# Sevens of w_down moved between the halves: four per column pair in the first, three and none in the second

## The chip, the cores and the metric

The kernel runs on one core of a Trainium2 chip. The metric is the device time of one execution in microseconds; of the kernel before there are three runs. One more execution was recorded by the hardware profiler, and all rows of the trace are from that one. The engines are named as in the profile: PE is TensorE, PEld its weight load, DVE VectorE, ACT ScalarE, POOL GpSimd, SP SyncE (which issues the loads).

## What is computed

A decoder layer for 256 tokens of width 2048, in float32: attention in two groups of heads with a combined input projection and an output projection, then a gated feed-forward part of width 5632. The change touches the last product of the second part, `y = g @ w_down`, and what surrounds it:

```python
h = rmsnorm(x, pre_ffn_g)
u = causal_dwconv(h @ w_up, conv_w, conv_b)          # (256, 11264)
gate, val = split(u, 2)
y = (gelu(gate) * val) @ w_down                      # (256, 5632) @ (5632, 2048)
x = x + rmsnorm(y, post_ffn_g)                       # the output
```

## The kernel before, in words

**Float32 by parts.** Each operand is split into a rounded high part and the low remainder, and a product is three matmuls: high by high, high by low, low by high (`products`, L973 for 512 columns, `mm3`, L284 for 256). The split of a weight block is a cast on ACT (into a `whi` buffer) and a subtraction on DVE (into `wlo`, called a low below): L118 and L121 for a whole load of 512 KB (128x1024), L287 and L288 for half of one (128x512). Loads come through SP's queue into five `raw` buffers; there are five `whi` and five `wlo` buffers too.

**The feed-forward part** runs in two halves of the width 5632, each of 22 row blocks of 128. Per half, first w_up, convolution and gate make 22 tiles `G` (11 rounds `g` of two); then w_down multiplies them. Four column blocks of 512 make the 2048 outputs; they are taken as two pairs, n=0 (blocks 0 and 1) and n=2 (blocks 2 and 3). Two tiles of 128 tokens (t=0, 1) by two column blocks are the four sums of a pair, in PSUM banks b, g (block n) and e, h (block n+1). They are added into `y_sb` by `down` (L963 on DVE; in the second half ACT squares the finished sum, L965, and POOL multiplies the gain; of the first column pair these multiplications are kept in the list `gains` and issued in the second pair).

**Fours and sevens.** A pair of row blocks (index u, 0 to 10) and one column block is a *four*: one load, one split, 12 matmuls. Both column blocks by fours are 24 matmuls. Instead, a *seven* takes the pair of row blocks and both column blocks at once as a 2x2 product of blocks by seven products instead of eight (Strassen's way): 21 matmuls, two loads, seven half splits, four differences of weight blocks on DVE (L1000 to L1003). The sums of activations that it needs are made beside w_up, on POOL, and split into the tile `sums`. Four of its seven products go to banks of their own, `shared` (a, c, d, f), and `fold` adds these into `y_sb` when the last seven of the pair is through. Three of the 11 pairs of row blocks (WIN = 3) are sevens in both column pairs of both halves; the loop over i has 8 turns, each a four for both column blocks, and at i = 0, 2, 4 a seven first, whose second part (`others`) comes after the fours. In the second half's fold three of the adds are on POOL (L1045, L1048, L1050).

**The tail.** In the second half, column block 3 isn't computed in the loop beside block 2 but after it (`tail`): there fours without a seven run through block 3, for the 8 row-block pairs that are no sevens. Its t=0 sum goes on in bank e. Its t=1 sum is made in two halves of 256 columns in two banks of their own, `b1`, so that the first half can be finished while the second is computed. These banks are opened by a matmul (L1108) whose result an ACT copy (L1109) replaces with `y_sb[:, 1, 1536:2048]`, the sum so far; the products L284 then add to it. For the last six row-block pairs the t=1 products are held back to the end, and the weights of two of them lie in the tile `rest`.

**Order.** PE's order is the program's. That of ACT, DVE, POOL and SP is set by a scheduler that goes by its own costs, up to the end of the tail's products, where the written order takes over.

## Time and profile before

| | |
|---|---|
| time, median of 3 runs | 1065.81 us (1065.45 to 1067.0) |
| profiled execution | 1066.15 us |
| its span, first to last instruction | 1064.4 us |
| mean granted TensorE clock | 0.996 |
| busy: PE, PEld | 1050.5 (99%), 913.8 (86%) us |
| busy: DVE, ACT, POOL | 813.9 (76%), 635.7 (60%), 255.6 (24%) us |
| first half's w_down on PE | about 575.9 to 692 us |
| second half's w_down with the tail, on PE | about 932 to 1056 us |
| second half's column pair n=2 without the tail | about 992 to 1026.5 us |
| loads of w_down | 88 of 512 KB, 4.7 us from issue to landing |
| second half's loads of x for the end, `x_end` | 2 of 1 MB, issued at 1022.41 and 1027.74 us |

Times of the trace are in us from the start of the span. A timeline row has start, duration, engine, line and operation, the tile written and those read, the shape, and in brackets how long the engine had been idle before and what it waited for last. A matmul's duration overlaps the next one's; the rate of a row of matmuls is read from start to start. PEclk is the granted clock, 1.00 being the whole. Where rows of one engine overlap (a cast of 1.05 us, and the next starts 0.95 later) the busy time counts the overlap once.

### The profile page before, as it was taken

The numbers are of one execution on the slowest core, as the hardware profiler recorded it, in microseconds if no ns is written. First come the engines' busy times: TensorE is split into PE (matmuls) and PEld (weight loads), VectorE is DVE, ScalarE is ACT, GpSimd is POOL, SyncE is SP. The second block draws the span as 40 slices with busy tenths as digits, with TensorE's granted clock in tenths as the row PEclk, the third lists the DMA queues.
The fourth block names the chain that finished last, engine by engine and source line by source line (L and its number), as shares of the span: only waits on it lengthen the run. The fifth ranks groups of instructions, "written<-read, shape, count | busy, mean of one in ns | idle before, by whom it ended". The sixth has DMA issues, their size and how long they took to land.

```text
span 1064.4 us, 16400 instructions
## 1 busy us (share of the span) xinstructions
PE 1050.5 (99%) x5920; PEld 913.8 (86%) x5920; DVE 813.9 (76%) x1340; ACT 635.7 (60%) x1124; POOL 255.6 (24%) x280
## 2 busy tenths in 40 slices
PE   9999999999999999999999999999999999999987
PEld 7889988888889888888888888888888888888866
DVE  5989868886568887777678887767877777788982
ACT  6776757767548666556565544455655656555650
POOL 3353245440122433112121000014312212102230
PEclk9999999999999999999999999999999999999989
DMA  8645666545866666666664666766666666557572
GB/s 290 191 128 174 181 192 212 173 154 160 298 222 201 220 200 202 190 198 198 193 185 137 213 210 203 243 190 185 182 204 194 196 190 198 156 181 241 162 259 79
DMA packets 165549, 207.09 MB, mean 195 GB/s; under 512 B 6844, under 2 KB 131036, under 8 KB 164444
## 3 DMA queue, kind: packets, MB, share of 16 engines
q1 hardware_dynamic: 165148, 205.65, 62.1%
q8 instruction: 46, 0.75, 0.3%
q10 hardware_dynamic: 320, 0.40, 0.1%
q14 instruction: 35, 0.29, 0.1%
HBM read 201.68 MB, written 4.21 MB: 193 GB/s over the span
## 4 chain that ended last, share of the span: by engine, by line
PE 91%; DVE 4%; issue 2%; ACT 1%; POOL 1%; DMA 1%; DVEq 0%; POOLq 0%; ACTq 0%
PE bank_acc L262 21%; PE bank_acc L973 15%; PE bank_att L262 15%; PE bank_acc L284 13%; PE bank_acc L269 11%; PE bank_att L269 8%; PE bank_att L973 2%; DVE wlo L121 1%; PE bank_att L450 1%; PE bank_att L485 1%; PE bank_att L494 1%; PE bank_acc L881 1%; DVE wlo L288 1%; PE bank_att L496 0%; DMA raw<-in_w_down_dram 0%
## 5 line engine op out<-in xcount | busy, mean ns | idle before, releaser
L121 DVE TENSOR_TENSOR wlo<-raw,whi 128x1024 fp32r<-128x1024 f32 (+3 forms) x333 | 404.6, 1227 | 137.6 <-ACT whi L118 130.7
L118 ACT CAST whi<-raw 128x1024 fp32r<-128x1024 f32 (+3 forms) x332 | 337.9, 1033 | 191.5 <-issue 100.2
L262 PE MATMUL bank_acc<-hT,whi 128*128 128x512 f32 x1024 | 245.6, 392 | 0.0
L262 PEld LDWEIGHTS bank_acc<-hT,whi 128*128 128x128 f32 x1024 | 188.2, 188 | 37.1
L857 POOL TENSOR_TENSOR u<-u,rowf 128x256 f32<-128x256 f32 x88 | 95.5, 1107 | 456.0 <-DVE u L856 453.0
L973 PE MATMUL bank_acc<-whi,G 128*128 128x512 f32 x520 | 167.9, 391 | 0.1
L262 PE MATMUL bank_att<-hT,whi 128*128 128x512 f32 x704 | 165.7, 390 | 0.0
L262 PEld LDWEIGHTS bank_att<-hT,whi 128*128 128x128 f32 x704 | 130.6, 188 | 26.2
L269 PEld LDWEIGHTS bank_acc<-hT,wlo 128*128 128x128 f32 x1024 | 123.4, 188 | 3.2
L269 PE MATMUL bank_acc<-hT,wlo 128*128 128x256 f32 x1024 | 125.7, 278 | 0.0
L973 PEld LDWEIGHTS bank_acc<-whi,G 128*128 128x128 f32 x520 | 98.2, 189 | 20.7 <-DVE y_sb L963 0.5
L973 PE MATMUL bank_acc<-wlo,G 128*128 128x512 f32 x260 | 101.8, 391 | 0.0
L269 PEld LDWEIGHTS bank_att<-hT,wlo 128*128 128x128 f32 x704 | 83.6, 188 | 1.9
L269 PE MATMUL bank_att<-hT,wlo 128*128 128x256 f32 x704 | 83.9, 277 | 0.0
L284 PE MATMUL bank_acc<-whi,oT 128*128 128x512 f32 (+1 forms) x272 | 81.8, 379 | 0.0
L287 ACT CAST whi<-raw 128x512 fp32r<-128x512 f32 x84 | 48.7, 618 | 36.1 <-PE bank_acc L973 21.2
L288 DVE TENSOR_TENSOR wlo<-raw,whi 128x512 fp32r<-128x512 f32 x84 | 60.6, 755 | 11.8 <-ACT whi L287 11.6
L284 PEld LDWEIGHTS bank_acc<-whi,oT 128*128 128x128 f32 x272 | 50.2, 188 | 9.3
L973 PEld LDWEIGHTS bank_acc<-wlo,G 128*128 128x128 f32 x260 | 49.1, 189 | 10.2 <-DVE wlo L121 0.3
L284 PE MATMUL bank_acc<-wlo,oT 128*128 128x512 f32 (+1 forms) x136 | 51.2, 377 | 0.0
L284 PE MATMUL bank_acc<-whi,hT 128*128 128x384 f32 (+1 forms) x192 | 46.9, 323 | 0.0
L859 ACT ACTIVATE yg<-u,cw 128x256 f32<-128x256 f32 x44 | 26.5, 602 | 32.4 <-POOL u L857 32.4
(250 smaller groups left out, 1286.7 us busy)
## 6 DMA issues: line engine op xcount, KB each, us to landing
raw<-in_w_up_dram SPq DMA_DIRECT2D x176, 512.0 KB, 4.5
raw<-in_w_down_dram SPq DMA_DIRECT2D x88, 512.0 KB, 4.7
raw<-in_w_in_dram SPq DMA_DIRECT2D x51, 512.0 KB, 4.9
raw<-in_w_out_dram SPq DMA_DIRECT2D x32, 512.0 KB, 4.7
raw<-in_w_in_dram SPq DMA_DIRECT2D x16, 384.0 KB, 3.3
cb<-c_dram SPq DMA_DIRECT2D x8, 256.0 KB, 4.2
x_sb<-in_x_dram SPq DMA_DIRECT2D x2, 1024.0 KB, 6.3
x_dram<-x_sb SPq DMA_DIRECT2D x2, 1024.0 KB, 5.8
```

The lines of the kernel that those rows point to most:

```text
L118: i1 = act.copy(hi[:, cs], raw[:, cs])
L121: i2 = dve.tensor_tensor(lo[:, cs], raw[:, cs], hi[:, cs].bitcast(F32), op=ALU.subtract)
L262: pe.matmul(b, hi[:, a, m * P:(m + 1) * P], hT[:, kt, 0:512], start=(kt == 0), stop=(last == (0, kt)))
L269: pe.matmul(b[:, 256:512], lo[:, a, m * P:(m + 1) * P], hT[:, u * 4 + a, 0:256], start=False, stop=(last == (1, u * 4 + a)))
L284: pe.matmul(b, a, r[:, cols], start=(first and i == 0), stop=(last and i == 2))
L287: act.copy(hi, src)
L288: dve.tensor_tensor(lo, src, hi.bitcast(F32), op=ALU.subtract)
L450: pe.matmul(sb[e][:, cs], a[r, t * P:(t + 1) * P], b[r, 0:nk], start=(n == 0), stop=(n == 2))
L485: pe.transpose(pb[:, i * P:(i + 1) * P], p[:, e, c:c + P], ident)
L857: pool.tensor_tensor(u[:, 2:258], u[:, 2:258], rowf, op=ALU.mult)
L859: act.activation(y, u[:, 2:258], AF.Identity, bias=cw[:, 3, ch:ch + 1], scale=cw[:, 2, ch:ch + 1])
L973: pe.matmul(b, x, r, start=b not in opened and not i, stop=closes and i == 2)
```

## The change

The number WIN gives way to a table, SEVENS, of the turns i at which a seven runs, for each half and column pair. In the first half there are four sevens in each column pair, at i = 0, 1, 3, 4 of 7 turns; in the second three in n=0 as before, and in n=2 none. So in the second half's n=2 there is no `fold` and no `shared` bank, the loop has 11 turns of one four each, and the tail has 11 row-block pairs instead of 8. The activation sums s1 to s4 all lie in `s` (s1 no longer overwrites a21 in the G tile), which makes their split 512 columns wide instead of 384. The second half's fold has all its adds on DVE, and the gains of the first column pair are issued at the turn of the last seven, or at i = 0 where there is none.

```diff
--- before.py
+++ after.py
@@ -25,7 +25,7 @@
 NEG = -1e30
 FHALF = 22
 HOLD = 6
-WIN = 3
+SEVENS = (((0, 1, 3, 4), (0, 1, 3, 4)), ((0, 2, 4), ()))
 LOW = (14, 4, 4, 4)
 ROOM = 112
 
@@ -908,8 +908,9 @@
         for half in range(2):
             G = [fp.tile([P, 512], F32R, tag="G", bufs=FHALF, name=f"G{j}")[:, 0:512]
                  for j in range(FHALF)]
+            most = max(len(at) for at in SEVENS[half])
             if half:
-                sums = main.tile([P, WIN, 768], F32R, tag="x", name="sums")
+                sums = main.tile([P, 4, 1024], F32R, tag="x", name="sums")
             for g in range(FHALF // 2):
                 c0 = (half * (FHALF // 2) + g) * 256
                 alt = (g + half) % 2
@@ -934,22 +935,23 @@
                     y = conv(bv[m], 44 + c0 // P + m, "yv")
                     dve.tensor_tensor(y, y, gates[m], op=ALU.mult)
                     ys.append(y)
-                if g < WIN:
+                if g < most:
                     if half == 0 and g == 0:
                         for t in range(2):
                             sp.dma_start(x_dram[t * P:(t + 1) * P, :], x_sb[:, t, :])
-                        sums = main.tile([P, WIN, 768], F32R, tag="x", name="sums")
+                        sums = main.tile([P, 4, 1024], F32R, tag="x", name="sums")
                     s = fp.tile([P, 512], F32, tag="s", name="s")
                     (a11, a21), (a12, a22) = [(y[:, 0:P], y[:, P:256]) for y in ys]
-                    pool.tensor_tensor(s[:, P:256], a11, a21, op=ALU.subtract)
-                    pool.tensor_tensor(a21, a21, a22, op=ALU.add)
-                    pool.tensor_tensor(s[:, 0:P], a21, a11, op=ALU.subtract)
-                    pool.tensor_tensor(s[:, 256:384], a12, s[:, 0:P], op=ALU.subtract)
+                    s1, s2, s3, s4 = (s[:, i * P:i * P + P] for i in range(4))
+                    pool.tensor_tensor(s1, a21, a22, op=ALU.add)
+                    pool.tensor_tensor(s2, s1, a11, op=ALU.subtract)
+                    pool.tensor_tensor(s3, a11, a21, op=ALU.subtract)
+                    pool.tensor_tensor(s4, a12, s2, op=ALU.subtract)
                 for m, y in enumerate(ys):
                     gt = G[g * 2 + m]
                     split(gt[:, 0:256], gt[:, 256:512], y)
-                if g < WIN:
-                    split(sums[:, g, 0:384], sums[:, g, 384:768], s[:, 0:384])
+                if g < most:
+                    split(sums[:, g, 0:512], sums[:, g, 512:1024], s)
             if half == 1:
                 rest = main.tile([P, KT, 512], F32R, tag="hT", name="rest")
                 gbf = fp.tile([P, D], F32, tag="gbc", name="gbc_ffn")
@@ -983,7 +985,7 @@
                 split(hi, lo, src)
                 return hi, lo
 
-            def seven(n, u, banks, opened):
+            def seven(n, u, last, banks, opened):
 
                 b, e, g, a, c, d, f = banks
                 k = half * FHALF + u * 2
@@ -991,8 +993,8 @@
                                for m in (n, n + 1)]
                 b11, b21, b12, b22 = (x[:, i * 512:i * 512 + 512] for x in (left, right)
                                       for i in range(2))
-                s2, s3, s4 = [(sums[:, u, i * P:i * P + P], sums[:, u, 384 + i * P:512 + i * P])
-                              for i in range(3)]
+                s1, s2, s3, s4 = [(sums[:, u, i * P:i * P + P],
+                                   sums[:, u, 512 + i * P:640 + i * P]) for i in range(4)]
                 dst = w_parts(UNIT, held=False)
                 w11 = split_512(dst, 0, b11)
                 w22 = split_512(dst, 1, b22)
@@ -1001,7 +1003,6 @@
                 dve.tensor_tensor(b12, b22, b12, op=ALU.subtract)
                 dve.tensor_tensor(b22, b22, b11, op=ALU.subtract)
                 dve.tensor_tensor(b21, b21, b22, op=ALU.subtract)
-                last = u == WIN - 1
                 products(a, parts_of(u * 2, 0), *w11, opened, last)
                 products(b, parts_of(u * 2 + 1, 0), *w21, opened)
                 products(e, s4, *w22, opened)
@@ -1013,7 +1014,7 @@
                     dst = w_parts(UNIT, held=False)
                     t2 = split_512(dst, 0, b22)
                     t4 = split_512(dst, 1, b21)
-                    products(d, parts_of(u * 2, 1), *t1, opened, last)
+                    products(d, s1, *t1, opened, last)
                     products(f, s3, *t3, opened, last)
                     products(c, s2, *t2, opened, last)
                     products(g, parts_of(u * 2 + 1, 1), *t4, opened)
@@ -1042,29 +1043,33 @@
                     act.copy(s, a)
                     dve.tensor_tensor(y11, a, y11, op=ALU.add)
                     dve.tensor_tensor(s, c, s, op=ALU.add)
-                    pool.tensor_tensor(y12, y12, s, op=ALU.add)
+                    dve.tensor_tensor(y12, y12, s, op=ALU.add)
                     dve.tensor_tensor(y12, d, y12, op=ALU.add)
                     dve.tensor_tensor(s, f, s, op=ALU.add)
-                    pool.tensor_tensor(y21, y21, s, op=ALU.add)
+                    dve.tensor_tensor(y21, y21, s, op=ALU.add)
                     dve.tensor_tensor(s, d, s, op=ALU.add)
-                    pool.tensor_tensor(y22, y22, s, op=ALU.add)
+                    dve.tensor_tensor(y22, y22, s, op=ALU.add)
 
             for n in (0, 2):
                 opened = []
                 tail = half and n
-                shared = [bank("att") for _ in range(4)]
+                at = SEVENS[half][n // 2]
+                shared = [bank("att") for _ in range(4 if at else 0)]
                 b, e, g = [bank() for _ in range(3)]
                 h = None if tail else bank()
-                for i in range(FHALF // 2 - WIN):
-                    others = (None if i % 2 or i > 2 * WIN - 2 else
-                              seven(n, i // 2, (b, e, g, *shared), opened))
-                    four(n, WIN + i, (b, g), opened)
+                for i in range(FHALF // 2 - len(at)):
+                    others = None
+                    if i in at:
+                        u = at.index(i)
+                        others = seven(n, u, u == len(at) - 1, (b, e, g, *shared), opened)
+                    four(n, len(at) + i, (b, g), opened)
                     if not tail:
-                        four(n + 1, WIN + i, (e, h), opened)
+                        four(n + 1, len(at) + i, (e, h), opened)
                     if others:
                         others()
-                    if i == 2 * WIN - 2:
+                    if at and i == at[-1]:
                         fold(n, *shared)
+                    if i == max((0, *at)):
                         for args, kw in gains:
                             pool.tensor_tensor(*args, **kw)
                 later_on = None if tail else lambda *args, **kw: gains.append((args, kw))
@@ -1107,7 +1112,7 @@
         for x, cs in zip(b1, halves):
             pe.matmul(x[:, cs], G[0][:, 0:P], G[0][:, 0:256], start=True, stop=False)
             act.copy(x[:, cs], y_sb[:, 1, 1536:2048][:, cs])
-        for u in range(WIN, FHALF // 2):
+        for u in range(len(at), FHALF // 2):
             hi, lo = w_unit(w_rows(w_down, FHALF + u * 2, 2, 1536, 512), 2, 512,
                             keep=(None, [rest[:, c:c + 2, :].rearrange("p a c -> p (a c)")
                                          for c in (4 * (u - LAST), 4 * (u - LAST) + 2)])
```

What moves, in the order of the engines' own programs (shapes without a note are those of the tile written).

ACT at the opening of the tail, before. The L118 rows are casts of weights, the L1109 rows the two copies into the `b1` banks, the L965 rows the squares of the two finished sums of column block 2:

```order
L1042 COPY s<-bank_att 128x512
L118 CAST whi<-raw 128x1024 x5
L118 CAST rest<-raw 128x1024 x2
L118 CAST whi<-raw 128x1024 x2
L1109 COPY bank_att<-y_sb 128x256
L965 ACTIVATE junk,ysq_3954<-y_sb 128x512
L1109 COPY bank_att<-y_sb 128x256
L965 ACTIVATE junk,ysq_3955<-y_sb 128x512
L118 CAST whi<-raw 128x1024 x2
L965 ACTIVATE junk,ysq_3954<-y_sb 128x512
```

And now, where the copies are L1114 and the squares L967:

```order
L118 CAST whi<-raw 128x1024 x9
L118 CAST rest<-raw 128x1024
L118 CAST whi<-raw 128x1024
L118 CAST rest<-raw 128x1024
L118 CAST whi<-raw 128x1024
L967 ACTIVATE junk,ysq_3954<-y_sb 128x512
L1114 COPY bank_att<-y_sb 128x256
L967 ACTIVATE junk,ysq_3955<-y_sb 128x512
L1114 COPY bank_att<-y_sb 128x256
L118 CAST whi<-raw 128x1024 x4
L967 ACTIVATE junk,ysq_3954<-y_sb 128x512
```

Before, one cast stood ahead of the first copy and one square ahead of the second; now a cast and a square stand ahead of the first copy, and the other square ahead of the second. The two casts into `rest` (weights of held-back row-block pairs) have a cast of another unit between them.

DVE in the first half's w_down, column pair n=0, before, from the first seven's second part to the third seven's first difference (L1000 to L1003 are the four differences of a seven, L288 the half lows of sevens, L121 the whole lows of fours):

```order
L121 TENSOR_TENSOR wlo<-raw,whi 128x1024 x2
L288 TENSOR_TENSOR wlo<-raw,whi 128x512 x3
L1000 TENSOR_TENSOR raw<-raw 128x512
L1001 TENSOR_TENSOR raw<-raw 128x512
L121 TENSOR_TENSOR wlo<-raw,whi 128x1024
L1002 TENSOR_TENSOR raw<-raw 128x512
L1003 TENSOR_TENSOR raw<-raw 128x512
L121 TENSOR_TENSOR wlo<-raw,whi 128x1024
L288 TENSOR_TENSOR wlo<-raw,whi 128x512 x4
L121 TENSOR_TENSOR wlo<-raw,whi 128x1024 x2
L288 TENSOR_TENSOR wlo<-raw,whi 128x512 x2
L1000 TENSOR_TENSOR raw<-raw 128x512
```

And now the same stretch, where the differences are L1002 to L1005:

```order
L288 TENSOR_TENSOR wlo<-raw,whi 128x512 x4
L1002 TENSOR_TENSOR raw<-raw 128x512
L121 TENSOR_TENSOR wlo<-raw,whi 128x1024
L1003 TENSOR_TENSOR raw<-raw 128x512
L121 TENSOR_TENSOR wlo<-raw,whi 128x1024
L1004 TENSOR_TENSOR raw<-raw 128x512
L288 TENSOR_TENSOR wlo<-raw,whi 128x512
L1005 TENSOR_TENSOR raw<-raw 128x512
L288 TENSOR_TENSOR wlo<-raw,whi 128x512 x3
L121 TENSOR_TENSOR wlo<-raw,whi 128x1024 x2
L288 TENSOR_TENSOR wlo<-raw,whi 128x512 x2
L1002 TENSOR_TENSOR raw<-raw 128x512
```

The two whole lows of the turn i = 1 that stood ahead of the second seven's half lows and differences are gone from there: its weights follow those of the first at once. Between the second and the third the row is as before.

SP in the second half, before:

```order
L72 DMA raw<-in_w_up_dram 128x4x256 x88
L72 DMA raw<-in_w_down_dram 128x2x512 x42
L1126 DMA x_end<-x_dram 128x2048
L72 DMA raw<-in_w_down_dram 128x2x512 x2
L1126 DMA x_end<-x_dram 128x2048
L1103 DMA out_dram<-y_sb 128x512 x6
```

And now:

```order
L72 DMA raw<-in_w_up_dram 128x4x256 x88
L72 DMA raw<-in_w_down_dram 128x2x512 x23
L1131 DMA x_end<-x_dram 128x2048
L72 DMA raw<-in_w_down_dram 128x2x512 x6
L1131 DMA x_end<-x_dram 128x2048
L72 DMA raw<-in_w_down_dram 128x2x512 x15
L1108 DMA out_dram<-y_sb 128x512 x6
```

The two loads of x_end move from behind 42 and 44 of the second half's 44 loads of w_down to behind 23 and 29.

## The prediction

> **What bounds the kernel now.** I read the page's head and its chain of waits first.
>
> ```profile
> span 1064.4 us, 16400 instructions
> PE 1050.5 (99%) x5920; PEld 913.8 (86%) x5920; DVE 813.9 (76%) x1340; ACT 635.7 (60%) x1124; POOL 255.6 (24%) x280
> PE 91%; DVE 4%; issue 2%; ACT 1%; POOL 1%; DMA 1%; DVEq 0%; POOLq 0%; ACTq 0%
> ```
>
> TensorE carries 91% of the chain, so time goes in two ways: more or fewer products, and places where TensorE stands still. For the second I looked at matmul starts in the two w_down stages, the only ones that the change touches. The first half's stage (575.9 to 692) has no place where starts lie further apart than their neighbours; the second half's has one large place, at the tail's opening (a first matmul L1108 into the bank, then products after a copy L1109). The timeline there, all engines in order of time (start, duration, engine and operation, idle time before it):
>
> ```profile
> 1026.08 3.43 DVE L121 TENSOR_TENSOR rest<-raw,rest 128x1024 fp32r<-128x1024 f32 x2
> 1026.24 2.19 POOL L1050 TENSOR_TENSOR y_sb<-y_sb,s 128x512 f32<-128x512 f32 x1 [0.80 <-DVE s L1049]
> 1026.29 0.39 PE L973 MATMUL bank_acc<-whi,G 128*128 128x512 f32 x1
> 1026.52 0.40 PE L1108 MATMUL bank_att<-G 128*128 128x256 f32 x2
> ...
> 1027.22 0.39 PE L973 MATMUL bank_acc<-whi,G 128*128 128x512 f32 x1
> 1028.46 0.38 ACT L1109 COPY bank_att<-y_sb 128x256 f32<-128x256 f32 x1
> 1028.89 0.39 PE L284 MATMUL bank_att<-whi,G 128*128 128x256 f32 x1 [1.28 <-ACT bank_att L1109]
> 1029.11 0.28 PE L284 MATMUL bank_att<-wlo,G 128*128 128x256 f32 x1
> 1029.23 0.28 PE L284 MATMUL bank_att<-whi,G 128*128 128x256 f32 x1
> ...
> 1030.57 1.27 DVE L963 TENSOR_TENSOR y_sb<-bank_acc,y_sb 128x512 f32<-128x512 f32 x2
> 1031.28 0.63 ACT L965 ACTIVATE junk<-y_sb 128x512 bf16<-128x512 f32 x1 [2.44 <-DVE y_sb L963]
> ...
> 1031.91 0.36 ACT L1109 COPY bank_att<-y_sb 128x256 f32<-128x256 f32 x1
> ...
> 1032.21 0.62 ACT L965 ACTIVATE junk<-y_sb 128x512 bf16<-128x512 f32 x1
> 1032.33 0.58 PE L284 MATMUL bank_att<-whi,G 128*128 128x256 f32 x1 [2.82 <-ACT bank_att L1109]
> ```
>
> The first copy waits for POOL's last add of the fold (1026.24, 2.19 us, so 1028.43). The second stands on ScalarE behind the square L965, and that behind DVE: two lows into `rest` that take 3.43 us while POOL works, another low, then the sum L963 at 1030.57. TensorE waits twice for a copy. The windows, cut where the granted clock changes (length, busy us of PE, PEld, DVE, ACT, POOL, then PEclk, DMA share, GB/s):
>
> ```profile
> 1027.62:1031.03 3.41, 0.62 (x3) 0.41 (x3) 3.41 (x3) 1.13 (x2) 0.81 (x1) 1.00 1.02 371
> 1031.03:1037.86 6.83, 5.53 (x20) 4.95 (x21) 4.33 (x7) 3.62 (x7) 4.26 (x2) 0.50 0.43 177
> 1054.92:1058.33 3.41, 1.56 (x13) 1.35 (x12) 0.98 (x3) 0.47 (x2) 0.55 (x1) 1.00 0.26 92
> 1058.33:1061.75 3.42, 0.00 (x0) 0.00 (x0) 2.39 (x5) 0.00 (x0) 0.00 (x0) 1.00 0.67 245
> ```
>
> After 3.41 us with TensorE busy for 0.62 the clock was at one half for 6.83 us; after 3.41 us with 1.56 busy (second to last row) it was still whole in the next.
>
> The rates, from a row of products without waits near the end:
>
> ```profile
> 1042.70 0.62 PE L973 MATMUL bank_acc<-whi,G 128*128 128x512 f32 x2
> ...
> 1047.46 0.39 PE L973 MATMUL bank_acc<-whi,G 128*128 128x512 f32 x1
> ...
> 1047.68 1.59 PE L284 MATMUL bank_att<-rest,G 128*128 128x256 f32 x12
> 1047.88 0.69 DVE L963 TENSOR_TENSOR y_sb<-bank_acc,y_sb 128x512 f32<-128x512 f32 x1 [9.64 <-PE bank_acc L973]
> ...
> 1049.12 0.28 PE L284 MATMUL bank_att<-whi,G 128*128 128x256 f32 x1
> ```
>
> From 1042.70 to 1047.46 lie 21 starts of 128x512: 0.227 us each. Twelve of 128x256 take 1.44 us: 0.120 each. From the start of a last product (1047.46) to the engine that waits for it (1047.88) it is 0.42.
>
> **The change, part by part.**
>
> *Products.* A seven takes 21 matmuls where two fours take 24. The first half gets two more (-6 matmuls), the second loses three (+9): +3 x 0.227 = **+0.68**. The tail now runs 11 row-block pairs instead of 8, and the three added run their t=1 part as two halves of 256: 36 matmuls at 0.120 (4.32) in the place of 18 at 0.227 (4.09): **+0.23**.
>
> *The fold that ended before the tail.* Column pair n=2 of the second half has no sevens, so no fold: y_sb[1, 1536:2048], which the copies read, is complete since the first half. Both waits as they are go. Counted from start to start: 1027.22 to 1028.89 is 1.67 for a slot of 0.23 (1.44 lost), 0.22 instead of 0.12 for the next (0.10), 1029.23 to 1032.33 is 3.10 for 0.12 (2.98): **-4.52**. With them goes the half clock: from 1032.33 to 1037.86 are 5.53 us, in which a 128x512 took 0.427 where it takes 0.227 (the rows of 0.42 and 0.43 between starts), so 5.53 x 0.200/0.427 = **-2.59**.
>
> ```profile
> 1033.14 0.63 PE L973 MATMUL bank_acc<-whi,G 128*128 128x512 f32 x1
> 1033.57 0.63 PE L973 MATMUL bank_acc<-wlo,G 128*128 128x512 f32 x1
> ```
>
> *The start of n=2.* There the seven of i=0 needed three converted weights at once, and TensorE lost a little: 992.44 to 993.24 is 0.80 for two slots of 0.227 (0.35 lost), 997.57 to 998.39 is 0.82 for three (0.14). With one four per i only one converted unit is needed per 12 x 0.227 = 2.72 us: **-0.49**.
>
> ```profile
> 992.44 0.97 PE L973 MATMUL bank_acc<-whi,G 128*128 128x512 f32 x2
> 993.24 0.40 PE L973 MATMUL bank_acc<-wlo,G 128*128 128x512 f32 x1
> ...
> 997.57 0.61 PE L973 MATMUL bank_acc<-whi,G 128*128 128x512 f32 x2
> ...
> 998.39 0.62 PE L973 MATMUL bank_acc<-whi,G 128*128 128x512 f32 x2
> ```
>
> *What is late next at the opening.* On ScalarE the two copies now stand behind a cast and a square each: cast, square, copy, square, copy. That cast writes a whi buffer that only the last product of n=2 sets free. How long a cast holds ScalarE, from one start to the next:
>
> ```profile
> 994.71 1.04 ACT L118 CAST whi<-raw 128x1024 fp32r<-128x1024 f32 x1
> 995.66 1.65 ACT L287 CAST whi<-raw 128x512 fp32r<-128x512 f32 x3
> ```
>
> Call the start of the opening matmul T (1026.52 above); the last product of n=2 starts at T-0.23. Cast at T-0.23+0.42 = T+0.19; square 0.95 later, T+1.14; copy 0.63 after it (1031.28 to 1031.91), T+1.77; TensorE 0.43 after that (1028.46 to 1028.89), T+2.20. Without a wait it would be there at 1027.22+0.23, T+0.93: 1.27 lost. The second square starts 0.30 after the first copy (1031.91 to 1032.21), T+2.07; its copy T+2.70, TensorE T+3.13. Three matmuls of 256 fill 0.46 of that (0.36 and 0.10 at the restart): 0.47 lost. With 0.10 at the second restart too, both cost 1.27+0.10+0.47+0.10 = **+1.94**. Bounds: nothing, if the cast's buffer is free sooner, and the 4.52 of today, if a load or a low is late; I take the value between because each of its links has a row. DVE's sums of n=2 need the same last product and 0.68 each, less than the cast, so they do not decide.
>
> The half clock should stay away: in a stretch of 3.41 us that holds both waits TensorE stands for 1.27+0.47 and works for about 1.6, as in the row with 1.56 that did not bring it, and far from the 0.62 that did.
>
> *Sevens at consecutive i in the first half* (0 and 1, 3 and 4). Cost nothing, if DVE hides it.
>
> ```profile
> L121 DVE TENSOR_TENSOR wlo<-raw,whi 128x1024 fp32r<-128x1024 f32 x35 | 42.7, 1222 | 16.9 <-ACT whi L118 16.8
> L288 DVE TENSOR_TENSOR wlo<-raw,whi 128x512 fp32r<-128x512 f32 x39 | 26.1, 705 | 8.4 <-ACT whi L287 8.3
> L1000 DVE TENSOR_TENSOR raw<-raw 128x512 f32<-128x512 f32 x5 | 3.4, 684 | 0.0
> 575.90:692.00 116.10, 116.10 (x514) 96.14 (x513) 91.72 (x120) 60.98 (x82) 1.69 (x2) 1.00 0.67 209
> ```
>
> An i with a seven is 21+24 matmuls, 45 x 0.227 = 10.2 us. For it DVE makes two whole lows, seven half ones and four differences: 2 x 1.22 + 7 x 0.705 + 4 x 0.684 = 10.1 us by mean durations, some 9.2 as rows overlap by about 0.1. So it keeps up by 1.0 per i, and an i without a seven (24 matmuls, 5.4 us; two lows, 2.4) gives 3 us back. In the stage as a whole four lows go, 14 half ones and 8 differences come: -4.9 + 9.9 + 5.5 = 10.5 us, so DVE rises from 91.7 of 116.1 us (79%) to some 102 of 114.4 (89%). If it does not keep up, the second of each pair of sevens is late, in four places.
>
> *Transfers and POOL at n=2.* The first x_end load moves up from behind 42 to behind 23 of the second half's 44 w_down loads, the second from 44 to 29, each 1 MB on SP's queue. In the 30 us of n=2 (11 x 2.72) SP must bring 11 loads of 512 KB and these two, 7.9 MB or 260 GB/s; the quoted window around 1029 shows 371 on the same queues. A load behind a waiting x_end has five raw buffers of lookahead, 2.72 us each. I count zero, at worst 1. The four gains on POOL run at the start of n=2, and a low beside a POOL operation took up to 2.3 us (3.43 for two, the first free in part), below 2.72: zero. The Trainium skill, "SBUF — State Buffer", section "Who interferes with whom", says that a DVE operation with two SBUF inputs waits for a whole GpSimd operation that reads SBUF. By that rule a low could wait for a whole operation of POOL, 2.2 us by the row at 1026.24, and end 3.4 after its cast, 0.7 more than a unit: the sum would be up to 1.4 higher for the two or three units beside the gains. The trace agrees that they disturb each other (3.43 us for two lows, where one without POOL takes 1.22).
>
> **Sum:** -4.52 - 2.59 - 0.49 + 0.68 + 0.23 + 1.94 = -4.75. The profiled execution took 1066.15 us, 1.7 around a span of 1064.4: 1061.4 after, with a span of 1059.7. The runs' median is 1065.81, 0.34 less; from there it is 1061.1. I forecast **1061.2 us**.
>
> **Rivals.**
> 1. *The opening costs nothing.* For it: copies, casts and squares are ordered by a scheduler and the cast's buffer may be free earlier. Then 1061.2 - 1.94 = 1059.3. Against: the cast waits for the last product of n=2, and stands ahead of both copies.
> 2. *The clock halves again.* The two new waits lie 0.46 us apart and may fall into one 3.41 us stretch. Such a stretch of 6.83 us costs up to 6.83 x 0.200/0.427 = 3.2; the one above cost 2.6. Time 1061.2 + 2.9 = 1064.1. Against: 1.56 busy kept the clock, and the longest new wait is under half of 2.98. The Trainium skill, "TensorE: Matmul & The Clock Gate", section "A second HAM failure mode: psum-queue depth-cycling", tells of a kernel in which short idle times between groups of matmuls alone made the clock swing. By that rule this rival decides, 1064.1; the trace speaks against it with the 1.56 row.
> 3. *DVE binds in the first half* (the other side). Its idle times in the stage, 16.9 + 8.4 us, stand before lows that wait for ScalarE's cast; they may be no slack but the latency of the chain load, cast, low, difference, cast. Over the 16 i of the two column pairs that is 1.6 us each. An i with a seven then takes DVE 10.1 + 1.6 = 11.7 us, 1.5 over TensorE's 10.2. This decides as soon as that sum passes 10.2, at the second seven of a pair, where no lighter i lies between: four places, 4 x 1.5 = 6.0; and as the late weights hold the buffers of the i behind, these four may be late as well, 12.0. Between them 9.0: 1070.2. For it: the 10.1 by mean durations. Against: today each i with a seven lost nothing, and five raw buffers let the second's loads start early.
> 4. *The opening is as late as now*, by a load behind x_end or a low behind POOL: +4.52 instead of +1.94, and the half clock's 2.6: 1061.2 + 2.6 + 2.6 = 1066.4. Against: DMA is not at its limit there, and no POOL work is left at the opening.
>
> **How the numbers follow.** Forecast 0.66, rival 1 0.10, rival 2 0.11, rival 3 0.08, rival 4 0.05. A difference of over 0.2%, 2.1 us, can be told from no change here: faster is below 1063.7, slower above 1067.9. Faster: 0.66 + 0.10 and a little of rival 2 = 0.78; within: the rest of 2 and all of 4, 0.14; slower: rival 3, 0.08. The forecast's own range is 1059.8 to 1063.2 (the opening between 0.6 and 2.9, a transfer or a low beside POOL up to 1). For 8 in 10 it takes in rival 1 and the near end of rival 2: 1059.1 to 1064.0.
>
> **What would show it.** Right: no halved clock before the kernel's last microseconds; at the opening two waits of TensorE for the copies, 1.0 to 1.5 and 0.3 to 0.6 us, behind cast, square, copy on ScalarE; matmul starts 0.227 apart throughout the first half's w_down and at the start of n=2. Wrong: PEclk below 1 near 1030 (rival 2), starts further apart at the second seven of a pair with DVE idle or late before it (rival 3), a wait above 2 us at the opening with a DMA or DVE named (rival 4). The forecast fails if the first half's stage, 252 x 2 x 0.227 = 114.4 us, takes over 2 us more.

## The result, and the profile after

The changed kernel takes 1061.71 us (median of 5 runs, 1061.52 to 1063.41), the kernel before 1066.04 (5 runs, 1065.45 to 1067.0): 0.9960 of it, 95% interval 0.9949 to 0.9972. The forecast was 1061.2. The profiled execution is the slowest of the five, 1063.41 us with a span of 1061.7; the next paragraphs show where its surplus lies.

The head of the page and the chain of waits of the changed kernel:

```profile
span 1061.7 us, 16409 instructions
PE 1050.2 (99%) x5941; PEld 914.6 (86%) x5941; DVE 803.8 (76%) x1330; ACT 634.0 (60%) x1119; POOL 252.1 (24%) x278
PE 90%; DVE 4%; DMA 2%; issue 2%; ACT 1%; POOL 0%; SPq 0%; DVEq 0%; POOLq 0%; ACTq 0%
```

The shares say next to nothing: TensorE is busy for 0.3 us less, and has 4% on DVE in its chain as before. What changed is seen when the program is cut into stages, each from the start of its first matmul to the start of the next stage's first. "First half" and "second half" below are the two w_down stages, the second with the tail and up to the start of the last matmul; both kernels have nearly the same work in the other rows.

| profiled execution, us | before | after | difference |
|---|---|---|---|
| start to the first w_down matmul | 575.87 | 577.49 | +1.62 |
| first half | 115.60 | 114.62 | -0.98 |
| second half's w_up | 240.68 | 240.68 | 0.00 |
| second half with the tail | 124.05 | 120.65 | -3.40 |
| last matmul to the end | 8.25 | 8.27 | +0.02 |

The +1.62 stands in the first 12 us. The timeline of PE there, after:

```profile
6.50 1.11 PE L309 MATMUL bank_acc<-ident,x_in 128*128 128x128 f32 x4 [0.39 <-DMA x_in<-in_x_dram]
7.27 2.05 PE L225 MATMUL bank_att<-hT,whi 128*128 128x512 f32 x4
```

And before:

```profile
6.13 1.08 PE L309 MATMUL bank_acc<-ident,x_in 128*128 128x128 f32 x4
6.89 1.23 PE L225 MATMUL bank_att<-hT,whi 128*128 128x512 f32 x4
```

Here the first load landed 0.4 us later, and the four matmuls of 128x512 then took 2.05 us instead of 1.23, and the next ones were slow as well. The change touches nothing of it, and the other executions of the changed kernel have spans of 1059.7 to 1060.3. So the executions are compared by stages from here on.

The tail's opening after the change, PE and ACT in order of time (rows of weight loads and of other engines are left out):

```profile
1020.28 0.39 PE L975 MATMUL bank_acc<-whi,G 128*128 128x512 f32 x1
1020.50 0.40 PE L1113 MATMUL bank_att<-G 128*128 128x256 f32 x2
1020.70 1.05 ACT L118 CAST whi<-raw 128x1024 fp32r<-128x1024 f32 x1
...
1021.21 0.39 PE L975 MATMUL bank_acc<-whi,G 128*128 128x512 f32 x1
...
1021.66 0.62 ACT L967 ACTIVATE junk<-y_sb 128x512 bf16<-128x512 f32 x1
...
1022.28 0.36 ACT L1114 COPY bank_att<-y_sb 128x256 f32<-128x256 f32 x1
...
1022.58 0.62 ACT L967 ACTIVATE junk<-y_sb 128x512 bf16<-128x512 f32 x1
1022.70 0.38 PE L284 MATMUL bank_att<-whi,G 128*128 128x256 f32 x1 [1.10 <-ACT bank_att L1114]
1022.92 0.28 PE L284 MATMUL bank_att<-wlo,G 128*128 128x256 f32 x1
...
1023.21 0.36 ACT L1114 COPY bank_att<-y_sb 128x256 f32<-128x256 f32 x1
1023.62 0.39 PE L284 MATMUL bank_att<-whi,G 128*128 128x256 f32 x1 [0.31 <-ACT bank_att L1114]
```

Cast, square, copy, square, copy, as forecast: with T = 1020.50 the cast starts at T+0.20, the square at T+1.16, the copy at T+1.78, PE at T+2.20; the second at T+3.12. And the windows, with the same columns as before:

```profile
1017.00:1024.00 7.00, 5.59 (x28) 4.29 (x27) 6.73 (x7) 5.75 (x10) 1.55 (x2) 1.00 0.75 227
1024.00:1030.00 6.00, 6.00 (x41) 5.43 (x40) 2.71 (x5) 2.11 (x2) 2.00 (x1) 1.00 0.38 145
577.40:692.10 114.70, 114.64 (x506) 94.58 (x505) 98.92 (x137) 64.32 (x91) 1.69 (x2) 1.00 0.66 210
```

The first two rows hold the opening and what follows it, the third the first half. PEclk stays at 1.00 through and behind the opening. In the first half DVE is busy 98.9 of 114.7 us (86%), and TensorE's busy time falls short of the window by 0.06 us. By matmul starts it lost 0.33 there, at one place, the start of the second column pair:

```profile
635.08 0.68 DVE L1005 TENSOR_TENSOR raw<-raw 128x512 f32<-128x512 f32 x1
...
635.68 1.22 DVE L121 TENSOR_TENSOR wlo<-raw,whi 128x1024 fp32r<-128x1024 f32 x1
...
636.81 1.28 DVE L965 TENSOR_TENSOR y_sb<-bank_acc,y_sb 128x512 f32<-128x512 f32 x2
...
637.10 0.95 PE L975 MATMUL bank_acc<-whi,G 128*128 128x512 f32 x2
637.55 0.19 PEld L975 LDWEIGHTS bank_acc<-whi,G 128*128 128x128 f32 x1 [0.49 <-DVE y_sb L965]
...
637.88 0.40 PE L975 MATMUL bank_acc<-wlo,G 128*128 128x512 f32 x1
```

Two matmuls there take 0.78 instead of 0.45 us, right behind the first of DVE's two sums that empty the banks of the first pair; the weight load of the second (PEld) names that sum as what it waited for. The sums stand on DVE behind a difference of the next seven and the low of a four.

### The profile page after: what moved, and what is told of

Read it like the earlier page. It is cut to its first block, busy times and chain, and to the rows that moved or that the text cites. A ratio compares the mean times of both kernels' runs of the same rounds, so it can differ in the third digit from the quotient of the medians.

```text
span 1061.7 us, 16409 instructions
## 1 busy us (share of the span) xinstructions
PE 1050.2 (99%) x5941; PEld 914.6 (86%) x5941; DVE 803.8 (76%) x1330; ACT 634.0 (60%) x1119; POOL 252.1 (24%) x278
## 4 chain that ended last, share of the span: by engine, by line
PE 90%; DVE 4%; DMA 2%; issue 2%; ACT 1%; POOL 0%; SPq 0%; DVEq 0%; POOLq 0%; ACTq 0%
PE bank_acc L262 21%; PE bank_att L262 15%; PE bank_acc L975 13%; PE bank_acc L284 13%; PE bank_acc L269 11%; PE bank_att L269 8%; DMA raw<-in_w_down_dram 2%; PE bank_att L975 2%; DVE wlo L121 1%; PE bank_att L450 1%; PE bank_att L485 1%; PE bank_att L494 1%; DVE wlo L288 1%; PE bank_att L225 1%; PE bank_acc L881 1%
## 5 line engine op out<-in xcount | busy, mean ns | idle before, releaser
L121 DVE TENSOR_TENSOR wlo<-raw,whi 128x1024 fp32r<-128x1024 f32 (+3 forms) x335 | 408.7, 1233 | 140.4 <-ACT whi L118 133.5
L118 ACT CAST whi<-raw 128x1024 fp32r<-128x1024 f32 (+3 forms) x334 | 340.8, 1035 | 196.7 <-issue 90.7
L287 ACT CAST whi<-raw 128x512 fp32r<-128x512 f32 x77 | 44.4, 621 | 27.2 <-DMA raw<-in_w_down_dram 14.5
L288 DVE TENSOR_TENSOR wlo<-raw,whi 128x512 fp32r<-128x512 f32 x77 | 52.7, 727 | 9.9 <-ACT whi L287 9.8
```

Source lines behind the costliest of these rows:

```text
L118: i1 = act.copy(hi[:, cs], raw[:, cs])
L121: i2 = dve.tensor_tensor(lo[:, cs], raw[:, cs], hi[:, cs].bitcast(F32), op=ALU.subtract)
L287: act.copy(hi, src)
L288: dve.tensor_tensor(lo, src, hi.bitcast(F32), op=ALU.subtract)
```

## The experiments

The theory: the second half's gain is due to the fold and the sevens' work that no longer end at the tail's opening (with the half clock that their waits brought), less nine matmuls and a new wait on ACT's order; the first half's is six matmuls less, which DVE hides. Rivals: that the fold was late only because it was on POOL; that loads were late; that the half clock has another cause; that DVE barely keeps up with sevens in sequence. All runs, stages from the profiled execution of each, times as medians; the ratio is to the kernel before in the same comparison, where its median lay between 1066.04 and 1066.36. Each edit below is shown against the changed kernel, unless another is named.

| kernel | first half | second half | time | ratio, 95% interval |
|---|---|---|---|---|
| before | 115.60 | 124.05 | 1066.04 | |
| after | 114.62 | 120.65 | 1061.71 | 0.9960 (0.9949 to 0.9972) |
| after, once more | 114.24 | 120.65 | 1061.81 | |
| second half's table alone | 115.60 | 120.65 | 1063.23 | 0.9974 (0.9964 to 0.9985) |
| first half's table alone, fold on DVE | 114.27 | 122.57 | 1063.87 | 0.9978 (0.9968 to 0.9987) |
| fold on DVE alone | 115.60 | 122.62 | 1064.90 | 0.9985 (0.9975 to 0.9995) |
| before, waits filled | 115.60 | 121.72 | 1064.58 | 0.9985 (0.9976 to 0.9994) |
| after, first half at 0, 1, 2, 3 | 114.47 | 120.88 | 1061.64 | 0.9956 (0.9940 to 0.9971) |
| after, early opening | 114.24 | 118.73 | 1060.12 | 0.9941 (0.9928 to 0.9953) |
| early opening, two sevens in n=2 | 114.24 | 117.19 | 1057.97 | 0.9923 (0.9911 to 0.9935) |
| the same, four sevens in n=0 | 114.70 | 119.41 | 1060.05 | 0.9940 (0.9926 to 0.9953) |
| early opening, n=2 at 0, 2, 4 | 114.24 | 121.63 | 1062.48 | 0.9963 (0.9947 to 0.9979) |
| early opening, n=2 at 0, 1, 3 | 115.15 | 119.78 | 1062.28 | 0.9968 (0.9957 to 0.9980) |

**The second half's table alone.**

```diff
-SEVENS = (((0, 1, 3, 4), (0, 1, 3, 4)), ((0, 2, 4), ()))
+SEVENS = (((0, 2, 4), (0, 2, 4)), ((0, 2, 4), ()))
```

> The table of the change for the second half alone; the first half keeps three sevens at i = 0, 2, 4 in each column pair. Theory (the gain is the fold that no longer stands before the tail, less nine matmuls): from the first to the last w_down matmul of the second half 120.65 us as in the changed kernel, against 124.05 before; the first half's stage 115.6 as before; time 3.4 under the kernel before, about 1062.6. Rival (the gain is the first half's): 124 in the second half, no gain.

Both stages came out to 0.01 us as the theory had them. So the halves do not act on each other, and 3.4 of the 4.4 us are the second half's. (The time is 0.6 over the expected one: 0.3 lay behind the last matmul in the profiled execution.)

**The fold on DVE alone**, with the old places of the sevens in both halves.

```diff
-SEVENS = (((0, 1, 3, 4), (0, 1, 3, 4)), ((0, 2, 4), ()))
+SEVENS = (((0, 2, 4), (0, 2, 4)), ((0, 2, 4), (0, 2, 4)))
```

> The old places of the sevens (i = 0, 2, 4 everywhere), only the fold's three adds of the second half on DVE instead of POOL. Theory (POOL's last add and the lows slowed by it held the copies back): no POOL work at the opening, two lows into rest in 2.3 us instead of 3.4, waits of 1.5 to 3 us in sum instead of 4.5, no half clock: the second half's w_down about 120 us, 3 to 5 under before, time about 1062. Rival (the opening is late by the fold's length wherever it runs, or by loads behind x_end): waits of 4 us and more, the clock halves, time about 1066.

Here the rival was right: waits of over 4 us, and the clock halves. POOL has no work ahead of the first copy, and that copy is even later. Its timeline:

```profile
1025.35 1.22 DVE L121 TENSOR_TENSOR rest<-raw,rest 128x1024 fp32r<-128x1024 f32 x1
1026.11 0.40 PE L1113 MATMUL bank_att<-G 128*128 128x256 f32 x2
...
1027.68 0.68 DVE L1051 TENSOR_TENSOR y_sb<-y_sb,s 128x512 f32<-128x512 f32 x1
...
1029.07 1.05 ACT L118 CAST whi<-raw 128x1024 fp32r<-128x1024 f32 x1 [2.68 <-DVE y_sb L965]
...
1030.64 0.36 ACT L1114 COPY bank_att<-y_sb 128x256 f32<-128x256 f32 x1
...
1031.06 0.39 PE L284 MATMUL bank_att<-whi,G 128*128 128x256 f32 x1 [3.86 <-ACT bank_att L1114]
```

The fold's last add ends at 1028.36, as late as POOL's did (1028.43), because its adds stand between lows of weights that came late. The chain of waits of this kernel says why these were late:

```profile
1011.85 1.82 DVE wlo L288 x3
1013.68 4.68 DMA raw<-in_w_down_dram
```

The last half lows of the last seven set the raw buffers free only at 1013.7, the load that waited for one lands 4.7 us later, and casts, lows and adds follow from there. The chain of the kernel before has the same two pieces:

```profile
1012.49 1.81 DVE wlo L288 x3
1014.32 4.65 DMA raw<-in_w_down_dram
```

So by the chain POOL was the last link of a delay, not its source. Whether loads behind `x_end`, the rival's other half, add to it was not tried. (The cast at 1029.07 is put down to a DVE sum that it doesn't need; which load or weight it waited for is not named here, and a later run shows its twin waiting for a load.) The waits cost 4.6 us in sum as before; the gain of 1.4 us is a half clock that is shorter (3.4 us of matmuls at 0.427 instead of 5.5, 1.0 less) and the missing wait at the start of n=2 (0.49). That wait is gone although the seven at i=0 stands there as before: DVE reaches its first two sums of n=0 at 988.03 instead of 988.66, with the adds of that pair's fold no longer on POOL.

**The first half's table alone**, with the second half as in the fold on DVE.

```diff
-SEVENS = (((0, 1, 3, 4), (0, 1, 3, 4)), ((0, 2, 4), ()))
+SEVENS = (((0, 1, 3, 4), (0, 1, 3, 4)), ((0, 2, 4), (0, 2, 4)))
```

> Four sevens per column pair in the first half as in the change, the old three in both column pairs of the second (with the fold on DVE). Theory: the first half's stage 114.6 instead of 115.6 us (six matmuls less, 1.36, and one short wait of 0.33 at the second column pair's start), the second half as in the run with only the fold moved; so 1.0 under that one. Rival (DVE binds at consecutive sevens and only this execution hid it): the stage at 116 or more.

114.27: 1.33 less than 115.60, the six matmuls and no wait at all. The second half is as long as with the fold on DVE (122.57 and 122.62), but by luck: its waits are shorter (3.3 and 0.1 us by starts instead of 4.0 and 0.5), and its half clock lasts 6.83 us instead of 3.41. Seven other profiled executions have the same table in the first half, and show how often the wait at the second column pair comes: four have none (114.24), and three are longer by 0.38, 0.46 and 0.91 us (the changed kernel, four sevens in n=0, n=2 at 0, 1, 3).

**The waits of the kernel before, filled with matmuls.** The edit is against the kernel before.

```diff
+        fill = bank("att")
...
-                    for x, cs in zip(b1, halves):
+                    for j, (x, cs) in enumerate(zip(b1, halves)):
+                        if k == WIN * 2:
+                            for _ in range((6, 12)[j]):
+                                pe.matmul(fill, G[0][:, 0:P], G[0], start=True, stop=True)
                         mm3(x[:, cs], G[k], 1, *args[1:], cs, False, False)
```

> The kernel before, with 6 and 12 more matmuls of 512 columns into a spare bank in the two waits of the tail's opening (1.36 and 2.72 us of work, less than the waits of 1.44 and 2.98). Theory (the half clock is brought by TensorE standing, and costs 2.6 by itself): the copies come no sooner, PEclk stays 1.00 to the last matmul, the second half's w_down 121.5 instead of 124.05 us, time 2.6 lower, about 1063.4. Rival (the clock falls for another reason, such as the transfers or the time since the start): PEclk 0.50 near 1031 again, time as before.

```profile
1027.45 1.53 PE L1124 MATMUL bank_att<-G 128*128 128x512 f32 x6
...
1029.09 0.37 ACT L1109 COPY bank_att<-y_sb 128x256 f32<-128x256 f32 x1
...
1029.52 0.39 PE L284 MATMUL bank_att<-whi,G 128*128 128x256 f32 x1 [0.54 <-ACT bank_att L1109]
...
1029.97 2.89 PE L1124 MATMUL bank_att<-G 128*128 128x512 f32 x12
...
1031.93 0.36 ACT L1109 COPY bank_att<-y_sb 128x256 f32<-128x256 f32 x1
...
1032.70 0.28 PE L284 MATMUL bank_att<-whi,G 128*128 128x256 f32 x1
```

The second copy comes when it did (1031.93 against 1031.91; the first is 0.63 later, behind a cast), and useless matmuls make the kernel faster: the windows of this kernel and of the one before, in this order:

```profile
1030.00:1040.00 10.00, 10.00 (x56) 8.66 (x55) 6.28 (x8) 3.64 (x7) 4.29 (x2) 1.00 0.40 153
```

```profile
1030.00:1040.00 10.00, 7.67 (x33) 6.87 (x34) 5.74 (x8) 3.62 (x7) 4.26 (x2) 0.66 0.41 159
```

The second half is 2.33 us shorter. Its second product starts at 1032.70 instead of 1032.33; as the stage began 0.11 later in this execution (932.25 against 932.15), that is 0.26 later. So the half clock alone is 2.33 + 0.26 = 2.59, as forecast. It comes from TensorE standing, and not from the transfers, which go on as before (153 and 159 GB/s). The medians differ by 1.8 us, less than the 2.6 expected: the profiled execution is the second fastest of its ten, and mean clocks of 0.994 to 0.997 in the 29 runs of the kernel before suggest that the half clock is not equally long in all of them.

**The opening two units earlier.**

```diff
+                    if tail and i == 8:
+                        b1 = [bank("att"), bank("att")]
+                        for x, cs in zip(b1, halves):
+                            pe.matmul(x[:, cs], G[0][:, 0:P], G[0][:, 0:256], start=True, stop=False)
+                            act.copy(x[:, cs], y_sb[:, 1, 1536:2048][:, cs])
                     if i == max((0, *at)):
...
-        b1 = [bank("att"), bank("att")]
-        for x, cs in zip(b1, halves):
-            pe.matmul(x[:, cs], G[0][:, 0:P], G[0][:, 0:256], start=True, stop=False)
-            act.copy(x[:, cs], y_sb[:, 1, 1536:2048][:, cs])
```

> The changed kernel, with the opening matmuls of the two b1 banks and their copies issued two units earlier in the column pair n=2, since y_sb[1, 1536:2048] is complete long before. Theory (the copies stand behind a cast and the squares on ACT, and this costs 1.9 us): no wait of PE for a copy, the second half's w_down 118.7 instead of 120.65 us, time 1.9 under the changed kernel, about 1059.8. Rival (the cast and its low are late anyway and the tail's products wait for them): the same 120.65.

```profile
1012.74 0.40 PE L1075 MATMUL bank_att<-G 128*128 128x256 f32 x2
...
1013.90 0.67 ACT L1076 COPY bank_att<-y_sb 128x256 f32<-128x256 f32 x2
...
1019.12 0.28 PE L284 MATMUL bank_att<-whi,G 128*128 128x256 f32 x1
```

The copies end at 1014.57, 4.5 us before they are needed. 118.73: 1.92 less than the changed kernel, so this is what its new wait cost; no matmul of the two w_down stages starts late any more.

**Two sevens in n=2 again**, with the opening after turn i = 6 of the 9. The edit is against the early opening.

```diff
-SEVENS = (((0, 1, 3, 4), (0, 1, 3, 4)), ((0, 2, 4), ()))
+SEVENS = (((0, 1, 3, 4), (0, 1, 3, 4)), ((0, 2, 4), (0, 2)))
...
-                    if tail and i == 8:
+                    if tail and i == 6:
```

> As early_open, and the second half's n=2 has two sevens again, at i = 0 and 2, with the fold at i = 2 of 9 turns and the opening four turns later. Theory (sevens there cost only where their fold and loads end close to the tail): six matmuls of 512 less, 1.36, and 24 instead of 36 more of 256, 0.16, against the 0.49 at the start of n=2 as in the kernel before: the second half's w_down about 117.7 us, time about 1058.8. Rival (a seven per turn of only one four keeps DVE, the raw buffers and so the loads late up to the tail, wherever the fold is): waits of over 2 us at the opening or before, 119 us or more.

117.19: 1.54 less than the early opening alone, which is the six matmuls (1.36) and the 0.16, and nothing was lost at the start of n=2. This is the fastest kernel, 1057.97 us, 3.7 under the changed one. The margin has become thin: the copies end at 1022.07 and are needed 1.4 us later.

```profile
1018.55 1.05 ACT L118 CAST rest<-raw 128x1024 fp32r<-128x1024 f32 x1 [5.45 <-DMA raw<-in_w_down_dram]
...
1021.40 0.67 ACT L1076 COPY bank_att<-y_sb 128x256 f32<-128x256 f32 x2
...
1023.47 0.28 PE L284 MATMUL bank_att<-whi,G 128*128 128x256 f32 x1
```

**Four sevens in the second half's n=0 too.** The edit is against the two sevens.

```diff
-SEVENS = (((0, 1, 3, 4), (0, 1, 3, 4)), ((0, 2, 4), (0, 2)))
+SEVENS = (((0, 1, 3, 4), (0, 1, 3, 4)), ((0, 1, 3, 4), (0, 2)))
```

> As two_sevens, and four sevens at i = 0, 1, 3, 4 in the second half's n=0 too. Theory (consecutive sevens beside two fours a turn are hidden, as in the first half): three matmuls less, 0.68: the second half's w_down 117.0, time about 1058.1. Rival (DVE, which also has the sums to add and three adds more in the fold there, falls behind): 118 or more with PE waiting at the second seven or at the start of n=2.

The rival was right: 2.2 us more than with three there, where 0.7 less were to be had.

```profile
991.79 7.57 POOL L1079 TENSOR_TENSOR y_sb<-y_sb,gbc_ffn 128x512 f32<-128x512 f32 x3
992.39 3.59 DVE L288 TENSOR_TENSOR wlo<-raw,whi 128x512 fp32r<-128x512 f32 x4
...
995.91 2.30 DVE L121 TENSOR_TENSOR wlo<-raw,whi 128x1024 fp32r<-128x1024 f32 x1
998.26 0.50 PE L975 MATMUL bank_acc<-wlo,G 128*128 128x512 f32 x1 [1.26 <-DVE wlo L121]
```

DVE reaches n=2 late, and there its lows meet the gains on POOL: four half lows take 3.59 us (0.9 each, where 0.60 is the pace without POOL) and a whole one 2.30. How much of it is the lateness and how much POOL was not separated.

**Sevens at four turns in a row.**

```diff
-SEVENS = (((0, 1, 3, 4), (0, 1, 3, 4)), ((0, 2, 4), ()))
+SEVENS = (((0, 1, 2, 3), (0, 1, 2, 3)), ((0, 2, 4), ()))
```

> The changed kernel with the four sevens of the first half at i = 0, 1, 2, 3: three follow directly on another. Theory (DVE needs some 9.2 us per turn with a seven, 1.0 under PE's 10.2): the first half's stage 114.3 to 114.6 us as with the change's places, time as the changed kernel, 1061.7. Rival (DVE needs 11.7 with its waits for casts): 1.5 late at each of three followers in two column pairs, 9 us: stage about 123, time about 1070.

114.47, 0.23 over the least, where the rival expected 9 us: at the third seven (598.6) TensorE waits 0.2 for a low. The second half is 0.23 longer too, as the cast ahead of the first copy stands behind one that waited for its load. In 39 us of the first column pair's four turns DVE is busy for 36.2:

```profile
577.00:616.00 39.00, 39.00 (x173) 32.04 (x172) 36.19 (x55) 24.36 (x39) 1.69 (x2) 1.00 0.61 187
```

So a turn with a seven needs some 9.5 us of DVE (36.2/39.0 of 10.2) against TensorE's 10.2, and the 9.2 of the forecast was close: rival 3 is excluded, though with little to spare.

**Three sevens in n=2 and the early opening.** First at the old places; both edits are against the two sevens.

```diff
-SEVENS = (((0, 1, 3, 4), (0, 1, 3, 4)), ((0, 2, 4), (0, 2)))
+SEVENS = (((0, 1, 3, 4), (0, 1, 3, 4)), ((0, 2, 4), (0, 2, 4)))
```

> As two_sevens, but the old three sevens in the second half's n=2, at i = 0, 2, 4 of 8, with the fold on DVE; the opening still stands after turn i = 6, one turn before the end. Theory (a fold that ends only at the tail, behind late casts, sets the opening): the copies come as late as in the run with only the fold moved, waits of some 4 us and a halved clock: the second half's w_down about 122, time about 1062. Rival (it was the place of the opening in TensorE's order that cost): no wait, 116.4, time about 1057.2.

```profile
1026.41 0.68 DVE L1051 TENSOR_TENSOR y_sb<-y_sb,s 128x512 f32<-128x512 f32 x1
...
1027.86 1.04 ACT L118 CAST whi<-raw 128x1024 fp32r<-128x1024 f32 x1 [2.34 <-DMA raw<-in_w_down_dram]
1028.81 0.67 ACT L1076 COPY bank_att<-y_sb 128x256 f32<-128x256 f32 x2
1029.23 0.48 PE L284 MATMUL bank_att<-whi,G 128*128 128x256 f32 x1 [3.42 <-ACT bank_att L1076]
```

The theory held: an earlier place of the opening is worth little (121.63, where the first half's table alone has 122.57) when the fold ends late and the cast ahead of the copies waits for a load. Here the trace names the load. With two sevens these waits were gone; but there the fold also stands two turns earlier, so the last seven's hold on the buffers and the place of its fold are not told apart. Its ten runs spread from 1058.71 to 1065.64.

Then the same with the sevens at i = 0, 1, 3 of n=2.

```diff
-SEVENS = (((0, 1, 3, 4), (0, 1, 3, 4)), ((0, 2, 4), (0, 2)))
+SEVENS = (((0, 1, 3, 4), (0, 1, 3, 4)), ((0, 2, 4), (0, 1, 3)))
```

> As two_sevens, with three sevens at i = 0, 1, 3 in the second half's n=2. Theory (in n=2 a turn has one four only, so a turn with a seven is 33 matmuls, 7.5 us, and DVE needs some 8.2 for it; its lateness moves the loads too): TensorE waits for weights at the second seven and the copies come late, 1 to 4 us more than with two sevens, the second half's w_down 118 to 121. Rival (the lookahead hides it): three matmuls less, 116.4 us.

119.78: PE loses 0.93 us in the second turn (at 1000.21, for the low of a four) and 2.38 at the opening, 2.28 for the copy and 0.10 at the restart. A turn of n=2 with a seven is too short for DVE, as reckoned, and the lateness ends at the tail. The clock stayed whole behind this wait.

**The changed kernel once more.**

> The changed kernel once more. Theory (the one short wait of 0.33 us in the first half's w_down, at the start of its second column pair, comes from loads and so differs between executions): the first half's stage 114.2 to 114.7, the second half's 120.65 with the two waits at the opening again, 1.3 and 0.5.

114.24 and 120.65 us: the opening repeats to 0.01 us, and the first half was without its short wait.

## Why the prediction was right, point by point

- *Products.* First half -1.36: four of the profiled executions show 114.24 against 115.60. Second half +2.04 and +0.23: as its whole came out at -3.40 with the other terms below, they stand; two sevens against none gave 1.54 for a reckoned 1.52.
- *Opening before, -4.52, and half clock, -2.59.* Both went. The half clock alone measured 2.59 by the filled waits.
- *Start of n=2, -0.49.* No matmul there starts late any more. The reason given, a seven that needs three weights at once, does not bear it: with the fold on DVE alone, and with two sevens, the seven at i=0 stands there and nothing is late. Most likely the fold of n=0 with its adds on POOL had made DVE late, and the change moved these as well.
- *New wait at the opening, +1.94.* Measured 1.26 + 0.10 + 0.47 + 0.10 = 1.93 by starts, and 1.92 by the early opening. Each link was within 0.03 us of its row in the forecast. The bound below, nothing, came true only with the copies issued elsewhere; with a cast that waited for its load (sevens at 0, 1, 2, 3) the wait was 0.23 longer.
- *Second half in sum:* forecast -3.39, measured -3.40. The two halves together gave -4.38 for a forecast of -4.75; the rest is the short wait of the next point.
- *Consecutive sevens cost nothing.* Nearly: 0 to 0.9 us, in the profiled execution 0.33. The step that was missed is the start of the second column pair: DVE's sums, which empty the banks, stand behind a difference of the next seven and the low of a four, and a slightly later DVE makes TensorE wait for a bank. What makes it later in some executions is not shown. The forecast looked for it at the second seven of a pair, where it isn't. It named DVE's share as 89%; it was 86%.
- *The clock stays whole.* So it did, in the three profiled executions with the waits of 1.26 and 0.47 (the change twice, and its second half alone), and with the 1.49 of the sevens at 0, 1, 2, 3.
- *Transfers and the gains beside the lows, zero.* So in the changed kernel. "No POOL work is left at the opening" was not so: POOL multiplies two gains there from 1022.45 on, and a low beside them took 2.30 us (1022.54); TensorE lost nothing by it. The gains' price is real where DVE has no slack, as four sevens in n=0 show.

One reason was wrong, though its number was right: the prediction read the opening's waits as those for POOL's last add and for two lows that POOL slowed ("The first copy waits for POOL's last add of the fold"). With the fold on DVE the first wait alone is 4.0 us, and both cost 4.6 as before. By the chain of waits the source is the last seven of n=2, which holds the raw buffers until 1014; POOL and DVE only passed the delay on. Had the change been the fold's move to DVE, this reasoning would have failed: it expected 3 to 5 us of that run, which gave 1.4. That the change left the late sevens out together with POOL's adds made the reason's error harmless. The rivals 1, 2, 3 and 4 did not come.

## What to carry to other kernels

Look behind the row that a wait names: the same delay was passed on by POOL in one kernel and by DVE in the next, and the chain of waits, followed back over 15 us, led to buffers that the work before had held. Where a wait is removed, write down the order of the engine that must then deliver, instruction by instruction, from the row that releases the first of them; that gave the new wait to 0.01 us, in the executions where no cast ahead waited for a load. And an operation whose input is ready early should be issued early in the order of the engine that waits for it: moving the opening changed nothing but its place and gave 1.9 us.

## What was not expected

Which stretches lose the clock is not told by the sum of the waits. PE standing 1.28 and 2.82 us (before) brought 6.83 us at one half, one wait of 3.11 and a short one (first half's table alone) 6.83 too; one of 3.86 and a short one (fold on DVE) brought 3.41, one of 3.42 (n=2 at 0, 2, 4) 3.41; one of 2.12 (n=2 at 0, 1, 3), with 2.28 lost by starts, brought none. The windows say more. They are cut where the clock changes, or counted in steps of 3.41 us from such a place:

| kernel | window, us | TensorE busy in it, of 3.41 us | clock in the next |
|---|---|---|---|
| n=2 at 0, 2, 4 | 1025.96 to 1029.37 | 0.14 | half |
| before | 1027.62 to 1031.03 | 0.62 | half |
| fold on DVE alone | 1028.69 to 1032.10 | 0.74 | half |
| first half's table alone | 1024.68 to 1028.09 | 1.23 | half |
| after | 1020.99 to 1024.40 | 2.00 | whole |
| n=2 at 0, 1, 3 | 1028.69 to 1032.10 | 2.22 | whole |

With the prediction's row of 1.56, which kept the clock, the two groups are apart, and so they are in all windows of the thirteen traces behind the first 12 us: from a whole clock, 1.23 us of TensorE work and less was followed by the half clock, and 1.56 and more never was. And the half clock lasted two windows where TensorE still waited in the first of them (busy for 2.11 us before, 2.48 with the first half's table alone), and one where it was busy for the whole of it. Where between 1.23 and 1.56 the border lies, and whether other kernels share it, these runs don't show. The forecast took the one length that its profile showed, 6.83, as the price.

Times spread more in kernels whose profiled execution has these waits: 1064.8 to 1068.4 for 29 runs of the kernel before (one run of a later series took 1070.4, with a mean clock of 0.946), and 1058.7 to 1065.6 for three sevens at 0, 2, 4. With the waits gone they lie closer: 1057.9 to 1058.5 for the fastest kernel, 1059.2 to 1060.5 for the early opening.

The slow start has the rate of the half clock: from 7.84 to 10.40 us matmuls of 128x512 columns of the changed kernel start 0.43 us apart. Yet PEclk reads 1.00 in a window from 6 to 11 us. That is no contradiction: the entries of the granted clock in its trace begin only at 10.64 us (7.03 before), just where the matmuls become fast, and ahead of the first entry the view counts a whole clock. Why the fast rate came 3.6 us later in this execution is not shown.
